# State space layer: last B matrices behind the tokens, tables in one piece on GpSimd, taps ahead of the second values, second turn between two products

## The chip, the cores and the metric

One core of a Trainium2 chip runs the whole program. The time is device microseconds (us) of one execution. The engines are TensorE (PE in the profile; PEld is its weight load), VectorE (DVE), ScalarE (ACT), GpSimd (POOL) and SyncE (SP). SP computes nothing here; it issues most of the DMAs, ACT and POOL issue some of their own. Each engine runs its instructions in the order in which they stand, so an instruction that waits holds up all behind it.

## The reference

Four residual layers over 256 tokens of width 1024, float32. Each layer has a token mixer, a cross-attention to 256 memory tokens and a gated MLP. Layer 2 (of 0 to 3) is the one that the change touches; its mixer is a diagonal complex state space model of 64 groups with 16 channels and 64 states each:

```python
def s5_mixer(h, a_re, a_im, log_dt, b_re, b_im, c_re, c_im, d, w_glu):
    ...
    b_bar = ((a_bar - 1.0) / lam)[..., None] * lax.complex(b_re.astype(f32), b_im.astype(f32))
    ...
    def chunk_step(state, u_blk):
        bu = jnp.einsum('bcgi,gpi->bcgp', u_blk.astype(jnp.complex64), b_bar)
        a_seq = jnp.broadcast_to(a_bar, bu.shape)
        _, xs = lax.associative_scan(_lin_rec_combine, (a_seq, bu), axis=1)
        xs = xs + a_pow[None] * state[:, None]
        y = jnp.real(jnp.einsum('bcgp,gip->bcgi', xs, c_mat))
        return xs[:, -1], y
    ...
    y = jax.nn.gelu(y).astype(h.dtype)
    val, gate = jnp.split(y @ w_glu, 2, axis=-1)
    return val * jax.nn.sigmoid(gate)
```

The memory's keys and values of the same layer (`mem_n @ wkv`) don't depend on the tokens.

## The kernel before, in words

**Products.** A float32 product is made of three matmuls on a high and a low part of both operands (`mm3`, L65 to L67). A weight therefore comes as `raw` (a tile of 1 MB in a ring of three buffers, DMA issued by SP at L88), is rounded by ACT into `whi` (L70) and the rest taken by DVE, or where the plan says `g` by POOL, into `wlo` (L71). The same two lines split every activation: `kh`/`kl`, `vh`/`vl`, `ah`/`al`.

**The state space layer.** Its matrices depend on no token and are built during the layers before, and kept in DRAM: `blD` (B, in four parts), `caD` (C times powers of A, four parts) and `tD` (taps of the convolution inside a block of eight tokens, four parts; `s5_spread`, L916, is the last copy that makes a part of it, two DMAs on POOL's queue for each part). With the tokens in hand `s5_mixer` (L933) does, in this order: the normalized tokens `u` go through eight DMAs of 128 KB into another layout, `uc` (four issued by SP, four by ACT, L962); they are reordered (`ur`, L986), transposed on PE and copied to `v` (L991, ACT and DVE in turn); PE multiplies them with B (`bl`, L1004) into the states' inputs `S` (L1008), transposes these into `SX` (L1030), and DVE scans over them: eight steps inside blocks (L1050 to L1061), then the carry over the blocks with the tables `tab8` (L1069, L1071), which POOL makes (`s5_eighths`, six L680 to L685 a round, L930). PE adds the taps (`taps_u`, L1080) and the carried states (`carry`, L1106) in four PSUM banks; the skip term (`uc` times `db`, L993 on POOL) is added on DVE (L1115), then Gelu (L1117, ACT), the turn back by PE (`turn`, L1123) with its split (L1126 ACT, L1127 DVE), and the GLU product (L1151) with eight weights of 1 MB. There are two halves of channels: `gelu(0)`, `turn(0)` give every second chunk of 128 channels, `gelu(1)`, `turn(1)` the others.

**What fills the waits.** The cross-attention's K (`k0` to `k3`) and V (`v0`, `v1`) products of the same layer are placed into the mixer by a table of names (`self.plan`, L1318 to L1325) and the calls of `self.fill`. `v0` stands at `scan0` and `v1` at `scan1`; a `+` only loads. v0's two PSUM banks are freed when DVE has taken `vl`.

**What sets the order.** A scheduler places each engine's instructions; `with self.behind(x)` keeps the instructions in the block behind `x` on the engine of `x`, and on no other engine. SP's DMAs use eight semaphores in turn, so that a DMA is issued only when the one that had its semaphore before has landed.

Of the kernel before, what the change touches and what calls it, by code (L numbers as in the profile page):

```python
# [36 lines left out]
class Trunk:  # L37
# [871 lines left out]
    def s5_spread(self, mm):  # L909

        if mm == 0:
            self.tD = self.dram.tile([4, P, 2, 8, P], F32, name="tD")
        kd = self.kD[:]
        for par in range(2):
            src = bass.AP(tensor=kd.tensor, offset=kd.offset + (2 * mm + par) * 256 * 240, ap=[[16, 8], [240 * 8, 16], [240, 8], [1, P]])
            self.nc.gpsimd.dma_start(self.tD[mm, :, par].rearrange("(s j) a k -> s j a k", s=8), src)  # L916

    def s5_eighths(self, sp):

        g = self.nc.gpsimd  # L920
        t = sp.tile([P, 3, GP, 8], F32, name="tab8")
        tmp = sp.tile([P, GP, 4], F32, name="tmp8")
        re, im = t[:, 0], t[:, 2]
        g.tensor_copy(re[:, :, 0], self.a8[:, 0, :])
        g.tensor_copy(im[:, :, 0], self.a8[:, 2, :])
        for by in (1, 2, 4):
            b = lambda y: y[:, :, by - 1 : by].to_broadcast([P, GP, by])
            new, old = slice(by, 2 * by), slice(0, by)
            self.cmul(g, re[:, :, new], im[:, :, new], re[:, :, old], im[:, :, old], b(re), b(im), tmp[:, :, 0:by])
        g.tensor_scalar_mul(t[:, 1], im, -1.0)  # L930
        return t

    def s5_mixer(self, l, sp):  # L933
        nc, a = self.nc, self.a
# [17 lines left out]
        for tt in range(TT):  # L952
            r = rs[tt]
            firsts = []
            for nh, f in enumerate((nc.vector.tensor_scalar_mul, nc.scalar.mul)):
                s = slice(512 * nh, 512 * (nh + 1))
# [11 lines left out]
        db = sp.tile([P, 2, 256], F32, name="db")  # L968
        with self.behind(last.ins):
            for i, row in enumerate((a["s5_d"][0], a["mix_norm_g"][l])):  # L970
                nc.sync.dma_start(db[:, i, :], bass.AP(tensor=row.tensor, offset=row.offset, ap=[[256, 4], [0, 32], [1, 256]]))
        with self.behind(self.powed):
            land(2, nc.gpsimd)
            land(3, nc.gpsimd)
            tab8 = self.s5_eighths(sp)
            nc.gpsimd.tensor_mul(db[:, 0, :], db[:, 0, :], db[:, 1, :])
        self.late = firsts
        self.fill("u")
        self.after = [chain, chain + [last.ins]]
        self.fill("u1")  # L980
        self.late = ()
# [103 lines left out]
        self.late = steps[-1:]  # L1085
        taps_u(0)
        taps_u(1)
        self.fill("scan1")
        self.late = ()
        for mm in (2, 3):  # L1090
            landed = taps_land(mm)
            taps_u(mm)

        def carry(mm):
            pool, tag = ((self.big, "xs"), (self.raw, "raw"), (self.raw, "raw"), (self.acts, "ah"))[mm]
            ou = pool.tile([P, 2, 4, 2, P], F32, tag=tag, name="ou")
            with self.behind(landed):
                nc.sync.dma_start(ou[:].rearrange("p m q x k -> p m (q x) k"), self.caD[:, 2 * mm : 2 * mm + 2])
            for m2 in range(2):
                m = 2 * mm + m2  # L1100
# [18 lines left out]
        def turn(h, yh):  # L1119
# [8 lines left out]
            return last  # L1128

        carry(0)  # L1130
        carry(1)
        y0, g0 = gelu(0)
        yT = self.act_pair()
        carry(2)
        done = carry(3)
        with self.behind(done):
            t0 = turn(0, y0)
        y1, _ = gelu(1)
        src = a["s5_w_glu"][0].rearrange("(q h p) n -> p h q n", p=P, h=2)
        for nh in range(2):  # L1140
            acc = self.accs() if nh else [self.bank() for _ in range(4)]
            for kh in range(2):
                for gate in (1, 0):
# [3 lines left out]
                    for tt in range(TT):  # L1147
                        for k in range(4):
                            c = 2 * k + kh
                            s = slice(tt * P, (tt + 1) * P)  # L1150
                            self.mm3(acc[2 * gate + tt][:], (yT[0][:, c, s], yT[1][:, c, s]), w(k, slice(0, 512)), c == 0, c == DC - 1)  # L1151
                if nh == 0 and kh == 0:
                    turn(1, y1)
            sgs = sp.tile([P, TT, 512], F32, tag="g", name="sg")
# [134 lines left out]
    def run(self, layers=range(DEPTH), parts="mcf"):  # L1289
# [14 lines left out]
        for l in layers:  # L1304
# [13 lines left out]
            elif l % 3 == 2:  # L1318
# [3 lines left out]
                self.plan((l, "u"), l, "k1 k2 k3")  # L1322
                self.plan((l, "u1"), l, "+v0dg")
                self.plan((l, "scan0"), l, "v0")
# [97 lines left out]
```

## Time and profile before

| | before |
|---|---|
| median of 3 runs | 1481.85 us (1478.66 to 1484.84) |
| the profiled execution | 1482.43 us, span 1480.7 us |
| mean granted TensorE clock | 0.982 |
| PE, DVE, ACT, POOL busy | 1426.4, 1096.5, 839.3, 124.3 us |
| the chain that ended last | PE 79%, DVE 9%, DMA 6%, ACT 3% |
| DMA | 279.74 MB, mean 189 GB/s |

All times below are microseconds from the start of the span. The mixer of layer 2 begins near 776 and its GLU product ends near 911. Between 700 and 800 PE is busy for 93.6 of 100 us, from 800 to 900 for 83.2 of 100 at a mean granted clock of 0.88; from 900 to 1400 for 97.3 to 100 of each 100.

### The profile page before, as it was taken

What the parts mean: (1) busy time and instruction counts of PE and PEld (TensorE: products, weight loads), DVE (VectorE), ACT (ScalarE), POOL (GpSimd) and SP (SyncE); (2) the same over time, 40 slices, a digit from 0 to 9 for tenths busy, and PEclk for the clock granted to TensorE, in tenths of its full rate; (3) what the DMA queues carried; (4) which work ended last, traced back from release to release, by engine and by line L of the source; (5) the groups of instructions that cost most, each with busy time, mean ns of one, the idle gap of its engine ahead of it and who ended that gap; (6) DMA issues with size and microseconds to landing.
All of it is one profiled execution on the core that took longest, in us unless ns stands there. A gap on an engine that the chain in (4) does not pass through costs nothing.

```text
span 1480.7 us, 25386 instructions
## 1 busy us (share of the span) xinstructions
PE 1426.4 (96%) x10354; PEld 1316.4 (89%) x10354; DVE 1096.5 (74%) x1722; ACT 839.3 (57%) x1351; POOL 124.3 (8%) x128
## 2 busy tenths in 40 slices
PE   7999999998999999999997789999999999999997
PEld 7897999998998989999987668999999999899996
DVE  6969888767886577978783857678677776677675
ACT  7654655547895455645453256565555565565553
POOL 3401000000000000111103500000000030000000
PEclk9999999999999999999998989999999999999999
DMA  7667656645444545776758675455555563465551
GB/s 261 229 164 220 222 199 206 219 135 166 151 149 161 187 148 191 250 225 221 235 192 234 238 233 170 158 171 199 183 187 182 178 210 136 143 220 171 189 181 43
DMA packets 205681, 279.74 MB, mean 189 GB/s; under 512 B 23740, under 2 KB 163132, under 8 KB 203644
## 3 DMA queue, kind: packets, MB, share of 16 engines
q1 hardware_dynamic: 198556, 260.46, 53.0%
q0 software_dynamic: 6432, 17.13, 3.5%
q8 instruction: 81, 1.33, 0.4%
q10 hardware_dynamic: 576, 0.52, 0.1%
q14 instruction: 36, 0.29, 0.1%
HBM read 264.24 MB, written 16.94 MB: 190 GB/s over the span
## 4 chain that ended last, share of the span: by engine, by line
PE 79%; DVE 9%; DMA 6%; ACT 3%; issue 1%; POOL 0%; SPq 0%; DVEq 0%; POOLq 0%; ACTq 0%
PE u L66 10%; PE u L67 10%; PE u L65 10%; PE mm L66 7%; PE mm L65 7%; PE mm L67 7%; PE acc L65 7%; PE acc L66 7%; PE acc L67 7%; DMA raw<-in_ffn_w_up_dram 3%; DVE wlo L71 2%; DMA raw<-in_xa_wkv_dram 2%; ACT whi L70 1%; DVE ug L1261 1%; DMA raw<-in_s_w_glu_dram 1%
## 5 line engine op out<-in xcount | busy, mean ns | idle before, releaser
L71 DVE TENSOR_TENSOR wlo<-raw,whi 128x1024 fp32r<-128x1024 f32 x430 | 519.3, 1220 | 157.0 <-ACT whi L70 148.4
L70 ACT CAST whi<-raw 128x1024 fp32r<-128x1024 f32 (+1 forms) x450 | 460.1, 1045 | 198.8 <-DMA raw<-in_ffn_w_up_dram 55.3
L65 PE MATMUL u<-ah,whi 128*128 128x256 f32 x1408 | 400.6, 285 | 1.7 <-DVE ug L1261 1.3
L66 PE MATMUL u<-al,whi 128*128 128x256 f32 x1408 | 399.8, 284 | 0.4 <-DVE al L71 0.4
L67 PE MATMUL u<-ah,wlo 128*128 128x256 f32 x1408 | 399.5, 284 | 0.0
L65 PEld LDWEIGHTS u<-ah,whi 128*128 128x128 f32 x1408 | 271.2, 193 | 6.3 <-issue 2.5
L66 PEld LDWEIGHTS u<-al,whi 128*128 128x128 f32 x1408 | 271.2, 193 | 3.4 <-DVE al L71 0.9
L67 PEld LDWEIGHTS u<-ah,wlo 128*128 128x128 f32 x1408 | 271.2, 193 | 0.0
L1261 DVE SCALAR_TENSOR_TENSOR ug<-u,cwT,ug 128x255 f32<-128x255 f32 x352 | 168.5, 480 | 101.3 <-ACT ug L1259 96.2
L1259 ACT ACTIVATE ug<-u,cwT 128x256 f32<-128x256 f32 x176 | 99.0, 563 | 185.6 <-PE u L67 125.0
L65 PE MATMUL acc<-whi,gg 128*128 128x512 f32 x352 | 138.0, 392 | 0.0
L66 PE MATMUL acc<-wlo,gg 128*128 128x512 f32 x352 | 137.9, 392 | 0.0
L67 PE MATMUL acc<-whi,gg 128*128 128x512 f32 x352 | 136.9, 389 | 0.0
L66 PE MATMUL mm<-al,whi 128*128 128x256 f32 x384 | 109.9, 286 | 0.1
L65 PE MATMUL mm<-ah,whi 128*128 128x256 f32 x384 | 109.8, 286 | 0.0
L67 PE MATMUL mm<-ah,wlo 128*128 128x256 f32 x384 | 109.4, 285 | 0.0
L176 POOL TENSOR_TENSOR r<-v,mhalf 128x1 f32<-128x1 f32 x28 | 22.7, 813 | 810.5 <-DVE v L172 678.7
L67 PEld LDWEIGHTS acc<-whi,gg 128*128 128x128 f32 x352 | 66.1, 188 | 14.4
L65 PEld LDWEIGHTS acc<-whi,gg 128*128 128x128 f32 x352 | 66.4, 189 | 11.7
L66 PEld LDWEIGHTS acc<-wlo,gg 128*128 128x128 f32 x352 | 66.4, 189 | 10.7
L66 PEld LDWEIGHTS mm<-al,whi 128*128 128x128 f32 x384 | 74.6, 194 | 0.8 <-DVE al L71 0.6
L65 PEld LDWEIGHTS mm<-ah,whi 128*128 128x128 f32 x384 | 74.6, 194 | 0.3 <-ACT ah L70 0.2
(355 smaller groups left out, 2564.9 us busy)
## 6 DMA issues: line engine op xcount, KB each, us to landing
raw<-in_ffn_w_up_dram SPq DMA_DIRECT2D x88, 1024.0 KB
raw<-in_ffn_w_down_dram SPq DMA_DIRECT2D x44, 1024.0 KB
raw<-in_xa_wkv_dram SPq DMA_DIRECT2D x30, 1024.0 KB
raw<-in_xa_wq_dram SPq DMA_DIRECT2D x16, 1024.0 KB
raw<-in_xa_wo_dram SPq DMA_DIRECT2D x16, 1024.0 KB
raw<-in_sb_w_qkv_dram SPq DMA_DIRECT2D x12, 1024.0 KB
raw<-in_s_w_glu_dram SPq DMA_DIRECT2D x8, 1024.0 KB
raw<-in_sb_w_o_dram SPq DMA_DIRECT2D x4, 1024.0 KB
```

The source lines that it names most:

```text
L65: mm(out, lh, rh, start=start, stop=False)
L66: mm(out, lh, rl, start=False, stop=False)
L67: self.multiplied = mm(out, ll, rh, start=False, stop=stop).ins
L70: x = self.nc.scalar.copy(hi, src)
L71: y = (eng or self.nc.vector).tensor_sub(lo, src, hi.bitcast(F32))
L176: self.powed = nc.gpsimd.tensor_tensor(r[:], v[:], self.mhalf[:], ALU.pow).ins
L1259: nc.scalar.activation(u[:, s, :], out, AF.Identity, bias=cw[3], scale=cw[2])
L1261: nc.vector.scalar_tensor_tensor(u[:, s, sh:], out[:, : T - sh], cw[2 - sh], u[:, s, sh:], ALU.mult, ALU.add)
```

## The change

Six edits, all in the mixer of layer 2:

- The last two parts of B (`land(2)`, `land(3)`) are issued by SP behind the token DMAs, ahead of `db`; before, POOL issued them.
- POOL makes the tables without a break, then the product of `db`, then issues both DMAs of the last `s5_spread`; the halves of a `+v0dg` load that POOL splits come behind these (`u2` in place of `u1`).
- The loads of taps 2 and 3 are issued ahead of v1's weights, and all four `taps_u` stand ahead of the v1 product; before, two of them stood behind it.
- The four loads of `caD` (`ou`) are issued together ahead of the first carry, the second of them into a tile of `acts` in place of `raw`.
- `turn(0)` stands behind `carry(2)`; before, behind `carry(3)`.
- `turn(1)` stands behind the first of the two products of the first GLU half (`gate` 1); before, behind both.

```diff
@@ s5_spread, s5_eighths
-            self.nc.gpsimd.dma_start(self.tD[mm, :, par].rearrange("(s j) a k -> s j a k", s=8), src)
+            self.spread = self.nc.gpsimd.dma_start(self.tD[mm, :, par].rearrange("(s j) a k -> s j a k", s=8), src).ins
...
-        g.tensor_scalar_mul(t[:, 1], im, -1.0)
+        self.eighths = g.tensor_scalar_mul(t[:, 1], im, -1.0).ins
@@ s5_mixer
         with self.behind(last.ins):
+            land(2)
+            land(3)
             for i, row in enumerate((a["s5_d"][0], a["mix_norm_g"][l])):
                 nc.sync.dma_start(db[:, i, :], ...
         with self.behind(self.powed):
-            land(2, nc.gpsimd)
-            land(3, nc.gpsimd)
             tab8 = self.s5_eighths(sp)
-            nc.gpsimd.tensor_mul(db[:, 0, :], db[:, 0, :], db[:, 1, :])
+        with self.behind(self.eighths):
+            spread_after = nc.gpsimd.tensor_mul(db[:, 0, :], db[:, 0, :], db[:, 1, :]).ins
         self.late = firsts
         self.fill("u")
         self.after = [chain, chain + [last.ins]]
-        self.fill("u1")
+        with self.behind(spread_after):
+            self.fill("u1")
+        with self.behind(self.spread):
+            self.fill("u2")
...
         self.late = steps[-1:]
-        taps_u(0)
-        taps_u(1)
+        for mm in (2, 3):
+            landed = taps_land(mm)
+        for mm in range(4):
+            taps_u(mm)
         self.fill("scan1")
         self.late = ()
-        for mm in (2, 3):
-            landed = taps_land(mm)
-            taps_u(mm)
-
-        def carry(mm):
-            pool, tag = ((self.big, "xs"), (self.raw, "raw"), (self.raw, "raw"), (self.acts, "ah"))[mm]
+
+        ous = []
+
+        def carried_land(mm):
+            pool, tag = ((self.big, "xs"), (self.acts, "al"), (self.raw, "raw"), (self.acts, "ah"))[mm]
             ou = pool.tile([P, 2, 4, 2, P], F32, tag=tag, name="ou")
             with self.behind(landed):
                 nc.sync.dma_start(ou[:].rearrange("p m q x k -> p m (q x) k"), self.caD[:, 2 * mm : 2 * mm + 2])
+            ous.append(ou)
+
+        def carry(mm):
+            ou = ous[mm]
...
+        for mm in range(4):
+            carried_land(mm)
         carry(0)
         carry(1)
         y0, g0 = gelu(0)
         yT = self.act_pair()
-        carry(2)
-        done = carry(3)
+        done = carry(2)
         with self.behind(done):
             t0 = turn(0, y0)
+        carry(3)
         y1, _ = gelu(1)
...
-                if nh == 0 and kh == 0:
-                    turn(1, y1)
+                    if (nh, kh, gate) == (0, 0, 1):
+                        turn(1, y1)
@@ run
-                self.plan((l, "u1"), l, "+v0dg")
+                self.plan((l, "u2"), l, "+v0dg")
```

The order that the scheduler makes of it differs only in this mixer; ahead of it and from the end of its GLU on, the same instructions stand in the same order on every engine. Line numbers of the changed program are 2 to 11 higher here (L986 is L990, L991 L995, L1008 L1012, L1016 L1020, L1030 L1034, L1098 L1103).

SP, from the token DMAs to the GLU's weights (`bl`: B, `tu`: taps, `ou`: the carry's matrices, `raw<-in_xa_wkv_dram`: weights of v0 and v1). Before:

```order
L962 DMA uc<-u 16x8x256 x4
L971 DMA db<-in_s_d_dram 128x1x256
L971 DMA db<-in_mix_norm_g_dram 128x1x256
L88 DMA raw<-in_xa_wkv_dram 128x4x512 x2
L1016 DMA tu<-tD 128x2048
L88 DMA raw<-in_xa_wkv_dram 128x4x512
L1016 DMA tu<-tD 128x2048
L88 DMA raw<-in_xa_wkv_dram 128x4x512
L1016 DMA tu<-tD 128x2048 x2
L1098 DMA ou<-caD 128x2048 x4
L88 DMA raw<-in_s_w_glu_dram 128x4x512 x3
```

And with the change:

```order
L962 DMA uc<-u 16x8x256 x4
L940 DMA bl<-blD 128x2048 x2
L973 DMA db<-in_s_d_dram 128x1x256
L973 DMA db<-in_mix_norm_g_dram 128x1x256
L88 DMA raw<-in_xa_wkv_dram 128x4x512 x2
L1020 DMA tu<-tD 128x2048 x4
L88 DMA raw<-in_xa_wkv_dram 128x4x512
L1103 DMA ou<-caD 128x2048
L88 DMA raw<-in_xa_wkv_dram 128x4x512
L1103 DMA ou<-caD 128x2048 x3
L88 DMA raw<-in_s_w_glu_dram 128x4x512 x4
```

Two B parts stand between the tokens and `db`; all four tap loads stand ahead of both weights of v1, which stood among them; the `ou` loads stand between and behind these weights.

POOL, behind the norm's last root (`tab`, `tmp`: the tables; the rounds of L680 to L685 go on below the piece). Before:

```order
L940 DMA bl<-blD 128x2048 x2
L924 COPY tab_8533<-a_1589 128x32
L925 COPY tab_8533<-a_1589 128x32
L916 DMA tD<-kD 128x8x128
L680 TENSOR_TENSOR tab_8533<-tab_8533 128x32
L681 TENSOR_TENSOR tmp_8534<-tab_8533 128x32
L683 TENSOR_TENSOR tab_8533<-tab_8533 128x32
L976 TENSOR_TENSOR db<-db 128x256
L682 TENSOR_TENSOR tab_8533<-tab_8533,tmp_8534 128x32
L71 TENSOR_TENSOR wlo<-raw,whi 128x1024
L684 TENSOR_TENSOR tmp_8534<-tab_8533 128x32
```

With the change, the end of the tables and what follows:

```order
L685 TENSOR_TENSOR tab_8533<-tab_8533,tmp_8534 128x32x4
L930 TENSOR_SCALAR tab_8533<-tab_8533 128x256
L977 TENSOR_TENSOR db<-db 128x256
L916 DMA tD<-kD 128x8x128 x2
L71 TENSOR_TENSOR wlo<-raw,whi 128x1024 x2
L997 TENSOR_TENSOR uc<-uc,db 128x2048
L1039 MEMSET X 128x64
L71 TENSOR_TENSOR wlo<-raw,whi 128x1024 x4
```

The tables moved ahead of the product of `db` and of every `wlo`; the first spread DMA moved from the third place behind the table's start to behind that product, the second now follows it at once.

ACT, from the token's reordering to the scan. Before:

```order
L986 COPY ur<-uc 128x512 x2
L991 COPY v<-mm 128x512
L70 CAST whi<-raw 128x1024 x2
L991 COPY v<-mm 128x512
L1008 COPY S<-mm 128x512
L70 CAST whi<-raw 128x1024 x2
L1008 COPY S<-mm 128x512
L1030 COPY SX<-mm 128x8x32
```

And with the change:

```order
L990 COPY ur<-uc 128x512 x2
L995 COPY v<-mm 128x512 x2
L1012 COPY S<-mm 128x512 x2
L70 CAST whi<-raw 128x1024 x2
L1034 COPY SX<-mm 128x8x32 x4
```

The `whi` of v0's weights moved behind ACT's copies of `v` and `S`. On DVE the two `wlo` of the same weight moved from ahead of its `S` copies to between its `SX` copies and the scan's first step.

## The prediction

> **What bounds it now.** The page's busy shares (PE 96%) say nothing about one stage, so I read the stretches first, cut where the waits fall: the state space mixer from its last K product (792) to the end of its GLU (911). Columns are busy time (and count) of PE, PEld, DVE, ACT and POOL, then granted clock, DMA share and GB/s.
>
> ```profile
> 792.00:813.00 21.00, 12.27 (x166) 10.61 (x165) 8.36 (x13) 9.62 (x16) 6.41 (x8) 0.76 0.84 244
> 813.00:847.00 34.00, 29.57 (x267) 23.77 (x273) 29.45 (x48) 7.84 (x10) 20.18 (x20) 0.90 0.64 233
> 847.00:876.00 29.00, 20.15 (x299) 15.79 (x284) 16.70 (x17) 15.53 (x16) 0.00 (x0) 0.91 0.87 295
> 876.00:911.00 35.00, 35.00 (x147) 28.68 (x147) 17.82 (x22) 14.07 (x20) 0.23 (x1) 0.93 0.50 159
> ```
>
> PE idles 8.7, 4.4 and 8.9 us there, and its clock is below full beside each hole: that is all the change can win. PE's waits between 785 and 900, longest first, name the holes (total, times, longest); the row at 806 below adds 2.2 us behind ACT's v copy:
>
> ```profile
> PE mm L990 <- ACT ur L986: 5.2, 1, 5.2
> PE mm L65 <- DVE vl L71: 4.4, 2, 2.4
> PE acc L1106 <- DMA ou<-caD: 3.5, 1, 3.5
> ```
>
> **Tokens and S.** The timelines of ACT and PE (start, duration, what; in brackets the idle time before it and what ended it), then the DMA queues from 780 to 798 (packets, MB, share of 16 engines):
>
> ```profile
> 792.63 0.58 ACT L70 CAST kh<-mm 128x512 fp32r<-128x512 f32 x1 [5.17 <-PE mm L67]
> 797.10 1.14 ACT L986 COPY ur<-uc 128x512 f32<-128x512 f32 x2 [3.89 <-DMA uc<-u]
> 803.60 1.99 ACT L70 CAST whi<-raw 128x1024 fp32r<-128x1024 f32 x2 [4.08 <-DMA raw<-in_xa_wkv_dram]
> 805.50 0.58 ACT L991 COPY v<-mm 128x512 f32<-128x512 f32 x1
> ...
> 797.78 3.68 PE L990 MATMUL mm<-ident,ur 128*128 128x128 f32 x16 [5.18 <-ACT ur L986]
> 806.13 3.55 PE L1004 MATMUL mm<-bl,v 128*32 128x128 f32 x64 [2.21 <-ACT v L991]
> 809.61 1.97 PE L1028 MATMUL mm<-ident,S 128*128 128x128 f32 x16
> ...
> q0 software_dynamic: 560, 2.63, 47.8%
> q10 hardware_dynamic: 576, 0.52, 12.3%
> ```
>
> The eight token transfers (uc, 1 MB) land at 797.1. Half of them went by q10 and took 12.3% of 18 us, 2.2 us of all engines, so all take 4.4. The bl transfers on GpSimd's queue (q0) took 8.6 us of the same time. With bl behind the tokens, uc lands between 785 and, if nothing changes, 797.1. I take any time before 792.6: then the third kh copy (792.63 + 0.58) is the next gate and ur starts at 793.2, 3.9 us earlier; the bounds are 3.9 and 0.
>
> In the Trainium skill, DMA: Bandwidth & Descriptors says that every DMA engine takes its queue rows in turn, packet by packet (Queues, rings and completion order), which agrees with q0 and q10 sharing the 18 us above. [...]
>
> The second v copy stood behind whi, which waited 4.08 us for a weight. ACT now runs v, v, S, S ahead of whi. Transposes at 793.8, 2.0 us at full clock (L1028's 1.97; the 3.68 is at half), the copies, and the second half of the S product starts near 797.2 instead of 806.13. It needs bl 2 and 3; these issue as tokens land, from about 786. The first row below is how long the two took today (the summary of tile bl); the others are DVE's timeline:
>
> ```profile
> DMA to landing us min/median/max: 6.7/9.0/11.3
> ...
> 804.68 2.36 DVE L71 TENSOR_TENSOR wlo<-raw,whi 128x1024 fp32r<-128x1024 f32 x2 [2.50 <-ACT whi L70]
> 813.35 1.22 DVE L1050 COPY X<-SX 128x256 f32<-128x256 f32 x1 [1.02 <-ACT SX L1030]
> 827.23 0.67 DVE L71 TENSOR_TENSOR vl<-mm,vh 128x512 fp32r<-128x512 f32 x1
> 831.40 0.51 DVE L1058 TENSOR_TENSOR two<-X,sc 128x192 f32<-128x192 f32 x1
> 842.43 0.62 DVE L1071 TENSOR_TENSOR X<-X,two 128x448 f32<-128x448 f32 x1
> ```
>
> So bl lands at 793 to 798: just in time. On SP it stands ahead of db and of v0's weights, 2 MB or 7.1 us at the 295 GB/s of the third stretch; but the same 2 MB shared the engines with them today, so I have v0's first weight land between 796 and today's 803.6. From 806.13 to the scan (813.35) is 7.2 us with two whi in it; DVE's two wlo (2.36), now ahead of the scan, run beside ACT's SX copies. Scan start: 797.2 + 7.2, 804.5 (8.8 earlier). If the weight lands no sooner than 803.6, whi and wlo push it to 808.0 (5.3 earlier).
>
> **Second values.** The v1 product needs v0's banks, freed by vl, and is now also behind all taps. POOL's timeline with the summary of tile tD (how long the spread took to land), then PE's and SP's:
>
> ```profile
> 800.89 0.72 POOL L976 TENSOR_TENSOR db<-db 128x256 f32<-128x256 f32 x1 [17.17 <-DMA db<-in_mix_norm_g_dram]
> 812.98 1.37 POOL L916 DMA_DIRECT2D tD<-kD  x1
> 829.56 2.36 POOL L71 TENSOR_TENSOR wlo<-raw,whi 128x1024 fp32r<-128x1024 f32 x1
> 832.42 0.87 POOL L930 TENSOR_SCALAR tab<-tab 128x256 f32<-128x256 f32 x1
> DMA to landing us min/median/max: 11.3/12.8/14.3
> ...
> 812.91 0.50 PE L65 MATMUL mm<-whi,mgh 128*128 128x512 f32 x1 [1.34 <-ACT SX L1030]
> 824.01 1.95 PE L1080 MATMUL acc<-tu,v 128*32 128x128 f32 x64
> 830.90 0.80 PE L65 MATMUL mm<-whi,mgh 128*128 128x512 f32 x1 [2.44 <-DVE vl L71]
> 844.53 1.95 PE L1080 MATMUL acc<-tu,v 128*32 128x128 f32 x64
> 825.71 0.34 SPq L1016 DMA_DIRECT2D tu<-tD  x1
> ```
>
> In the scan, vl comes 18.05 us (813.35 to 831.40) less two vl, 17 us, after its start: 821.5, first bank 822.2. The chain that I think ends later is on POOL and SP. The tables, whose last piece ends at 833.3 today, just ahead of their first use, run in one piece and cost nothing: they fit in the 17.17 us that POOL stood idle waiting for db. Behind them comes the db product, whose db now stands behind bl on SP: it lands between 794 and today's 800.9; then 0.72 and two spreads of 1.37 (today the second goes out at 812.98), 797.9 to 804.3; landing 11.3 to 14.3 later, 809 to 818.6. SP holds the last taps' load until then, and everything behind it: v1's weights, ou, GLU. Middle: tu(3) issues at 810.7 (825.71 today) and lands 6.7 us later (bl's least, the same 1 MB), 817.4. The v0 product starts near 803.6 with its first wlo, takes 11.1 us (812.91 to 824.01), and three taps 2.9: PE is there at 817.6, so the taps' move costs nothing; without that cover it costs what tu(3) is late. v1's first weight is 1 MB more, 3.6 us at 295 GB/s, then whi 1.0 and POOL's wlo 2.36: v1 starts at 824.4, 6.5 earlier, and no earlier than 822.2; with the late ends, 818.6 + 9.0 + 7.0 = 834.6, 3.7 later than now.
>
> **Carry, first turn.** v1 takes (830.90 to 844.53) 13.6 us as now (its half clock spell included): carry at 838.0; the scan ends at 804.5 + 29.7 = 834.2, and the four ou, now issued ahead, lie under v1, so the 3.5 us wait goes. The timelines from there on, and two stretches with the granted clock (next to the last two numbers):
>
> ```profile
> 846.41 2.03 PE L1106 MATMUL acc<-ou,X 64*32 64x128 f32 x128
> 849.86 1.06 ACT L1117 ACTIVATE uc<-uc 128x1024 f32<-128x1024 f32 x1 [4.64 <-DVE uc L1115]
> 855.42 1.96 PE L1123 MATMUL yt<-ident,uc 128*128 128x128 f32 x8
> 859.06 0.50 PE L65 MATMUL mm<-whi,ah 128*128 128x512 f32 x1 [1.68 <-ACT ah L1126]
> 870.62 1.04 PE L1123 MATMUL yt<-ident,uc 128*128 128x128 f32 x8
> 875.20 0.79 PE L65 MATMUL mm<-whi,ah 128*128 128x512 f32 x1 [1.43 <-ACT ah L1126]
> 875.00:881.00 6.00, 5.80 (x14) 4.54 (x15) 2.62 (x3) 2.28 (x3) 0.00 (x0) 0.50 0.66 183
> 806.00:808.00 2.00, 1.87 (x36) 1.74 (x40) 1.64 (x2) 2.00 (x4) 0.42 (x1) 0.51 0.22 90
> ```
>
> From carry to the end of gelu is 4.5 us (846.41 to 850.92), from the turn to the GLU 3.6: GLU at 838.0 + 8.1 = 846.1, 12.9 earlier.
>
> **Second turn.** It ended at 871.7, the product went on at 875.20 (3.5), and six microseconds at clock 0.50 cost 2.9 more. Between two products, its copies lie under 24 matmuls, 5.8 us (half of 859.06 to 870.62). Gelu 2 stands on ACT behind a GLU weight whose load waits for carry 2 (841 + 6.7 to 9.0, whi, gelu: 850 to 852); the first product ends at 851.9, so the cover barely holds. Without it, up to 3.5 us comes back. I take 6.4.
>
> **Sum.** 12.9 + 6.4 = 19.3 us. Against it one half clock spell, 2.9 us: in the row at 806 a wait of 2.21 us was enough for clock 0.51, and the carry, gelu and first turn still leave gaps of 1 to 2 us. That gives 16.4 off the execution's own 1482.43 (span 1480.7, 1.7 around it), so 1466.0; the execution lay 0.6 over the median of the runs, so against the median 1465 us. From 911 on no engine's order changes, and PE is full there, so what is won stays won.
>
> In the Trainium skill, TensorE: Matmul & The Clock Gate (Part 1) lets the clock fall after an idle window of about 3.4 us. By that the gaps stay at full clock and the sum is 19.3, 1462.5; the trace's 2.21 us speaks against it.
>
> **Rivals.** Data no earlier: the same 16 engines move the same bytes, tokens at 797.1, scan at 808.0. vl frees v1 at 825.7, 5.2 earlier; GLU 11.6 earlier, and with 6.4 - 2.9 the time is 1467. For it: DMA share 0.84 in the first stretch; against: half the bytes were q0's. Late spread: the late ends above, v1 at 834.6, the GLU at 856.3, 2.8 earlier, and with 6.4 - 2.9: 1475.5. For it: db waited 17 us; against: both spreads go out before today's second. Slower: the same chain, longer. GLU comes 13.7 + 13.6 + 8.1 = 35.4 us after tu(3) issues; with 6.4 - 2.9 won later, the two kernels are level when tu(3) issues at 827.3; at 837 the time is 1491. db would have to land after 809; nothing shows that. No effect: some wait that I don't see (a GLU weight, a bank) refills the holes, 1480.
>
> **Chances.** Forecast 0.50, data no earlier 0.15, late spread 0.17, slower 0.08, no effect 0.10. About 0.5% (7.4 us) is what a measurement tells from no change: faster 0.75 (with 0.10 of late spread), same 0.17, slower 0.08. The range goes from 1457 (v1 at 822.2, no half clock at all) to 1478 (late spread, second turn uncovered).
>
> **What would show it.** ur at 793, scan by 805, tu(3) issued before 812, v1 by 825, carry without a wait for ou, GLU near 846, no PE wait at the second turn. I am wrong if SP still waits for tD past 820 or ACT's whi holds the SX copies.

## The result, and the profile after

| | before | changed |
|---|---|---|
| median (range), first comparison, 5 runs each | 1479.22 us (1475.88 to 1484.84) | 1467.85 us (1466.19 to 1470.14) |
| ratio, 95% interval | | 0.9921 (0.9902 to 0.9941) |
| median (range), second comparison, 11 and 6 runs | 1479.15 us (1474.74 to 1485.54) | 1465.39 us (1463.80 to 1469.24) |
| ratio, 95% interval | | 0.9905 (0.9884 to 0.9927) |
| profiled execution: span, mean granted clock | 1480.7 us, 0.982 | 1465.8 us, 0.988 |

The change is 11 to 14 us faster; the forecast was 1465 us. Whether it was right for its reasons is another question, and for that the whole-program times are too coarse. I therefore look at one stage alone: from the start of the last `kh` copy on ACT (792.63 in the first profile of before) to the end of the last addition to `h` of this mixer. Both kernels were profiled twice. The stretches of the stage, in the order before, before again, changed, changed again (columns: start:end, length, busy us and count of PE, PEld, DVE, ACT, POOL, then granted clock, DMA share, GB/s):

```profile
792.63:912.15 119.52, 96.97 (x856) 78.80 (x856) 73.44 (x100) 48.04 (x62) 27.16 (x27) 0.89 0.68 226
```
```profile
791.65:908.27 116.62, 94.74 (x856) 77.45 (x856) 73.62 (x100) 48.14 (x62) 27.21 (x27) 0.88 0.69 232
```
```profile
793.93:897.34 103.41, 89.44 (x856) 73.50 (x856) 73.14 (x100) 48.10 (x62) 22.86 (x12) 0.93 0.78 273
```
```profile
796.83:899.33 102.50, 89.10 (x856) 72.80 (x856) 73.25 (x100) 48.24 (x62) 22.93 (x12) 0.95 0.78 276
```

The stage is 16.1 us shorter in the first pair and 14.1 in the second. What to see here: length less PE busy is PE's idle time, 22.6 and 21.9 us before, 14.0 and 13.4 after, so 8.5 us of waits are gone. The other 5.6 to 7.5 us are PE *busy* time, with the same 856 records on both sides: the same products ran at a higher granted clock (0.88 to 0.89 before, 0.93 to 0.95 after). So 40 to 47% of what the stage won is clock. The clock records of the four traces bear this out: half of the time that PE was busy at clock 0.50 is 11.7, 10.0, 4.7 and 4.1 us, and PE's busy time less that is 85.3, 84.8, 84.7 and 85.0 us, the same on both sides.

The same moments in all four profiles, in us after the last `kh` copy, beside the forecast (its times less 792.63):

| | before | before again | forecast | changed | changed again |
|---|---|---|---|---|---|
| `ur` starts | 4.5 | 5.2 | 0.6 | 0.5 | 0.5 |
| v0 product starts | 20.3 | 19.2 | 11.0 | 14.5 | 14.5 |
| scan starts | 20.7 | 19.6 | 11.9 (at worst 15.4) | 14.9 | 15.0 |
| tu(3) issued | 33.1 | 33.7 | 18.1 (at worst 26.0) | 24.6 | 24.6 |
| v1 runs, its waits behind it | 38.3 | 37.3 | 31.8 | 35.7 | 35.8 |
| carry | 53.8 | 53.0 | 45.4 | 49.4 | 48.5 |
| GLU | 66.4 | 66.8 | 53.5 | 57.0 | 56.1 |
| end of the stage | 119.5 | 116.6 | 103.1 | 103.4 | 102.5 |

The end is where it was forecast, what lies between is not. PE's waits of the changed kernel between 785 and 900, as for before:

```profile
PE mm L65 <- ACT SX L1034: 5.7, 1, 5.7
PE mm L65 <- ACT whi L70: 2.4, 1, 2.4
PE mm L66 <- POOL wlo L71: 1.9, 1, 1.9
...
PE mm L994 <- ACT ur L990: 1.2, 1, 1.2
```

Gone are `ur` (5.2, now 1.2), `vl` (4.4) and `ou` (3.5). New are 5.7 us ahead of the v0 product and 2.4 and 1.9 inside v1. ACT's timeline, with DVE's scan start, names the first:

```profile
793.93 0.58 ACT L70 CAST kh<-mm 128x512 fp32r<-128x512 f32 x1 [5.17 <-PE mm L67]
794.41 1.14 ACT L990 COPY ur<-uc 128x512 f32<-128x512 f32 x2
800.04 0.58 ACT L1012 COPY S<-mm 128x512 f32<-128x512 f32 x1 [1.16 <-PE mm L1008]
804.99 1.99 ACT L70 CAST whi<-raw 128x1024 fp32r<-128x1024 f32 x2 [4.36 <-DMA raw<-in_xa_wkv_dram]
806.89 1.96 ACT L1034 COPY SX<-mm 128x256 f32<-128x256 f32 x4
...
808.87 0.42 DVE L1054 COPY X<-SX 128x256 f32<-128x256 f32 x1 [0.45 <-ACT SX L1034]
```

`ur` no longer waits for the tokens, and ACT has done its copies of `v` and `S` by 800.6 (DVE its own by 801.6). Then ACT stands 4.36 us in `whi` for v0's first weight, with the SX copies behind it in order. POOL and SP, then SP's longest waits for the tap loads and weights:

```profile
802.52 0.72 POOL L977 TENSOR_TENSOR db<-db 128x256 f32<-128x256 f32 x1 [13.30 <-DMA db<-in_mix_norm_g_dram]
803.18 2.68 POOL L916 DMA_DIRECT2D tD<-kD  x2
...
818.49 0.32 SPq L1020 DMA_DIRECT2D tu<-tD  x1
818.92 0.38 SPq L88 DMA_DIRECT2D raw<-in_xa_wkv_dram  x1
823.98 0.38 SPq L88 DMA_DIRECT2D raw<-in_xa_wkv_dram  x1
...
SPq L1020 <- DMA tD<-kD: 14.3, 1, 14.3
SPq L88 <- PE acc L1084: 4.0, 1, 4.0
```

POOL waits for `db` until 802.5, the spreads go out behind it, SP stands 14.3 us for `tD`, and v1's first weight goes out only then; the second waits 4.0 more, until the tap product has freed its ring buffer. PE from there on:

```profile
827.15 0.49 PE L65 MATMUL mm<-whi,mgh 128*128 128x512 f32 x1 [2.35 <-ACT whi L70]
829.59 0.79 PE L66 MATMUL mm<-wlo,mgh 128*128 128x512 f32 x1 [1.94 <-POOL wlo L71]
843.33 2.85 PE L1115 MATMUL acc<-ou,X 64*32 64x128 f32 x186
847.56 0.65 PE L1115 MATMUL acc<-ou,X 64*32 64x128 f32 x26 [1.38 <-issue]
848.14 1.09 PE L1132 MATMUL yt<-ident,uc 128*128 128x128 f32 x8
850.93 0.50 PE L65 MATMUL mm<-whi,ah 128*128 128x512 f32 x1 [0.86 <-ACT ah L1135]
856.98 1.03 PE L1132 MATMUL yt<-ident,uc 128*128 128x128 f32 x8
```

Carry to GLU is 7.6 us (12.7 and 13.9 before), the turns run at full clock (1.09 and 1.03 for eight transposes, 1.96 for the first before), and no wait follows the second turn.

### The profile page after: what moved, and what is told of

Read it like the earlier page. It is cut to its first block, busy times and chain, and to the rows that moved or that the text cites. A ratio compares the mean times of both kernels' runs of the same rounds, so it can differ in the third digit from the quotient of the medians.

```text
span 1465.8 us, 25388 instructions
## 1 busy us (share of the span) xinstructions
PE 1418.3 (97%) x10354; PEld 1311.3 (89%) x10354; DVE 1096.4 (75%) x1722; ACT 839.3 (57%) x1351; POOL 123.3 (8%) x126
## 3 DMA queue, kind: packets, MB, share of 16 engines
q1 hardware_dynamic: 198844, 262.56, 53.8%
## 4 chain that ended last, share of the span: by engine, by line
PE 78%; DVE 10%; DMA 6%; ACT 3%; issue 2%; POOL 0%; SPq 0%; DVEq 0%; POOLq 0%; ACTq 0%
PE u L66 9%; PE u L67 9%; PE u L65 9%; PE mm L66 8%; PE mm L67 8%; PE mm L65 8%; PE acc L65 7%; PE acc L66 7%; PE acc L67 7%; DMA raw<-in_ffn_w_up_dram 3%; DVE wlo L71 3%; DMA raw<-in_xa_wkv_dram 2%; ACT whi L70 2%; DVE ug L1272 2%; DVE h L435 1%
## 5 line engine op out<-in xcount | busy, mean ns | idle before, releaser
L176 POOL TENSOR_TENSOR r<-v,mhalf 128x1 f32<-128x1 f32 x28 | 22.6, 808 | 790.9 <-DVE v L172 678.9
L67 PEld LDWEIGHTS acc<-whi,gg 128*128 128x128 f32 x352 | 66.1, 188 | 14.3
L65 PEld LDWEIGHTS acc<-whi,gg 128*128 128x128 f32 x352 | 66.4, 189 | 11.7
L66 PEld LDWEIGHTS acc<-wlo,gg 128*128 128x128 f32 x352 | 66.4, 189 | 10.8
L65 PE MATMUL mm<-mgh,whi 128*128 128x256 f32 x256 | 73.5, 287 | 1.0 <-ACT whi L70 1.0
```

Source lines behind the costliest of these rows:

```text
L65: mm(out, lh, rh, start=start, stop=False)
L66: mm(out, lh, rl, start=False, stop=False)
L67: self.multiplied = mm(out, ll, rh, start=False, stop=stop).ins
L176: self.powed = nc.gpsimd.tensor_tensor(r[:], v[:], self.mhalf[:], ALU.pow).ins
```

## The experiments

In each the stage was read from one profile and the time from several runs. Ratios are to the kernel before; the stage and its moments are in us after the last `kh` copy.

| kernel | v0 | scan | v1, first | carry | GLU | stage | PE idle | ratio (95%) |
|---|---|---|---|---|---|---|---|---|
| before, again | 19.2 | 19.6 | 34.4 | 53.0 | 66.8 | 116.6 | 21.9 | (one run) |
| changed, again | 14.5 | 15.0 | 33.3 | 48.5 | 56.1 | 102.5 | 13.4 | 0.9905 (0.9884 to 0.9927) |
| second turn only | 18.9 | 19.4 | 34.1 | 52.3 | 64.2 | 113.0 | 21.3 | 0.9968 (0.9955 to 0.9982) |
| copies before weight | 12.1 | 10.5 | 33.2 | 48.4 | 55.9 | 102.4 | 13.1 | 0.9908 (0.9892 to 0.9924) |
| `db` first | 16.3 | 16.7 | 33.9 | 48.8 | 57.4 | 103.8 | 15.0 | 0.9915 (0.9898 to 0.9931) |
| B parts on POOL | 17.5 | 18.0 | 35.3 | 48.0 | 55.9 | 102.3 | 13.8 | 0.9916 (0.9901 to 0.9931) |
| tap in u's buffer | 14.4 | 14.9 | 33.2 | 48.0 | 55.7 | 101.9 | 13.7 | 0.9919 (0.9894 to 0.9944) |
| all four | 12.8 | 11.9 | 31.3 | 43.4 | 54.6 | 101.2 | 12.5 | 0.9901 (0.9881 to 0.9921) |
| taps behind v1 | 14.5 | 15.0 | 32.1 | 46.7 | 58.6 | 105.6 | 14.4 | 0.9932 (0.9919 to 0.9946) |
| first turn behind carry | 14.5 | 14.9 | 33.2 | 48.4 | 56.7 | 106.1 | 15.8 | 0.9929 (0.9912 to 0.9946) |
| B on POOL, order free | 18.2 | 18.6 | 39.1 | 51.7 | 59.2 | 105.7 | 16.0 | 0.9907 (0.9892 to 0.9923) |
| half the bytes | 16.0 | 15.1 | 34.5 | 46.9 | 55.4 | 102.3 | 10.1 | 0.9894 (0.9877 to 0.9910) |

### Both kernels once more

> The kernel before, once more, for a second profile. From the start of the last kh copy (792.63 in the first profile) to the end of the last addition to h of this mixer (912.15) lie 119.5 us before and 103.4 us after the change: 16.1 us, against 11.4 us between the medians. Theory: the stage is stable within 1 us and the rest lies ahead of it, in code that no edit touches (the stage starts at 793 to 797 in the other profiles): 118.5 to 120.5 us here. Rival: the first profile fell on a long stage, and the stage is 3 to 5 us shorter here.

> The changed kernel, once more, for a second profile and more times on one chip. Theory: the same stage 102.5 to 104.5 us long; ratio to the kernel before 0.990 to 0.994. Rival, as above: a stage 2 us or more off, which would make differences of 1 to 2 us between single profiles worth nothing.

Measured: 116.6 and 102.5. The changed kernel's stage repeats within 1 us, that of before does not: 2.9 us, of which 2.2 are PE busy time. So differences of 1 to 2 us between single profiles carry nothing, and part of before's cost is clock that comes and goes. The stage itself starts anywhere between 791.7 and 796.8 in the fourteen profiles; behind it, 567 to 569 us follow in all of them. From the first token DMA to the last `kh` copy it is 12.4 to 12.5 us in every profile, so no edit moves the start. The scatter arises ahead of the mixer, in code that is the same in all: one ACT instruction there starts between 729.1 and 731.3, a later one between 766.2 and 771.4. Why it scatters stays open; it is why the medians and the stages of single profiles need not agree to 3 us.

### The second turn alone

```diff
 (kernel before)
-                if nh == 0 and kh == 0:
-                    turn(1, y1)
+                    if (nh, kh, gate) == (0, 0, 1):
+                        turn(1, y1)
```

> The kernel before, with one edit of the six: the second turn stands between the two products of the first GLU half. Theory (the prediction's step): the 3.5 us wait of PE at the second turn and the half-clock spell behind it (2.9 us) both go, 6.4 us less than before, and no PE wait stands behind the second turn's transposes. Rival one, the clock falls anyway: 3.5 us less. Rival two, the turn's copies are not covered by the other product: 0 to 1 us less. If 6.4 comes out, the other five edits together are worth only some 5 of the 11.4 us between the two kernels.

Measured: 4.7 us less in time (2.7 to 6.7), 6.5 and 3.6 in the stage against the two profiles of before. The GLU's first product and the second turn on PE, then two stretches of that product with the clock (next to the last two numbers):

```profile
858.44 0.80 PE L65 MATMUL mm<-whi,ah 128*128 128x512 f32 x1 [3.18 <-ACT ah L1126]
...
867.05 1.03 PE L1123 MATMUL yt<-ident,uc 128*128 128x128 f32 x8
```
```profile
858.00:861.00 3.00, 2.56 (x6) 2.10 (x7) 3.00 (x3) 3.00 (x4) 0.00 (x0) 0.50 0.90 355
864.00:867.00 3.00, 3.00 (x14) 2.45 (x14) 1.70 (x2) 0.00 (x0) 0.00 (x0) 1.00 1.00 341
```

No wait follows 867.05, so the cover holds. Half clock did not leave the GLU, though: it now follows the 3.18 us wait at the *first* turn. The edit takes the wait away for certain and the spell only if nothing else brings one. It is the one edit of the six that was tried alone on the kernel before, and its worth shows in the times.

### The copies ahead of v0's weight

v0's splits are emitted behind the SX copies and held there; the rest of the order stays.

```diff
+        with self.behind(self.spread, *copied[-2:]):   # the last SX copies on ACT and DVE
+            for f in deferred:                         # the splits of v0's two weights
+                f()
```

> The changed kernel, but ACT and DVE split v0's weights (whi, wlo) behind all SX copies, not ahead of them. In the changed kernel ACT stood 4.4 us in whi for v0's first weight with the SX copies behind it. Theory: the scan starts near 804 instead of 808.9 and the v0 product near 806 instead of 808.4, but v1 still starts when its own weight lands (near 827), since SP issues that weight only behind the last taps' load, and this one waits for tD: 0 to 1 us less than the changed kernel. Rival: the start of the scan or of the v0 product sets the end: 2.3 to 4.5 us less.

DVE's scan start and PE's starts of v0 and v1:

```profile
803.97 0.39 DVE L1067 COPY X<-SX 128x256 f32<-128x256 f32 x1 [1.00 <-ACT SX L1042]
...
805.52 1.22 PE L65 MATMUL mm<-whi,mgh 128*128 128x512 f32 x2 [3.27 <-ACT whi L70]
826.61 0.80 PE L65 MATMUL mm<-whi,mgh 128*128 128x512 f32 x1 [2.84 <-ACT whi L70]
```

The scan came 4.4 us earlier and v0 2.4, and v1 started where it does in the changed kernel, 33.2 after the `kh` copy, now with a longer wait for its weight. The time is the changed kernel's within the intervals. The missed scan start of the forecast was thus not what cost the carry.

### `db` before the tokens

```diff
         land(0)        # the two db loads now stand ahead of this
...
         with self.behind(last.ins):
             land(2)
             land(3)
-            for i, row in enumerate((a["s5_d"][0], a["mix_norm_g"][l])):
-                nc.sync.dma_start(db[:, i, :], ...
```

> The changed kernel, but SP issues the two small db loads with the first B parts, before the tokens, not behind them and two B parts. Theory: the db product on POOL follows the tables at 789 instead of 802.5, both spread DMAs go out by 793 and land by 807, SP no longer stands 14.3 us for tD; the next gate for v1's first weight is its buffer, which POOL's wlo of v0 frees at 816, against the 818.9 of the changed kernel: v1 starts 2 to 3 us earlier and the time is 2 to 3 us less than the changed kernel's. Rival: the spread's 1 MB then shares the engines with the tokens and B parts (full there already), what comes earlier on one side is late on the other: 0 to 2 us more.

SP's issue of v1's first weight and PE's start of v0:

```profile
819.00 0.38 SPq L88 DMA_DIRECT2D raw<-in_xa_wkv_dram  x1
...
812.92 0.80 PE L65 MATMUL mm<-whi,mgh 128*128 128x512 f32 x1 [6.57 <-ACT SX L1044]
```

The last `kh` copy starts at 796.67 here, so v1's weight went out at 22.3 instead of 25.0, as reckoned, and PE no longer waited for it. But v0 started 1.7 us later (its weight came at 11.6 instead of 11.1, and two of DVE's SX copies stand behind `wlo` in this kernel), and v1 not before 33.9: the rival. Two gates, each about as late as the other, hide each other's removal.

### B's last parts on POOL's queue

```diff
         with self.behind(last.ins):
-            land(2)
-            land(3)
...
         with self.behind(self.powed):
+            land(2, nc.gpsimd)
+            land(3, nc.gpsimd)
```

> The changed kernel, but POOL issues the last two B parts on its own queue beside the tokens, as before the change; ACT's and DVE's order is held to that of the changed kernel. The prediction priced the tokens' earlier landing at 3.9 us. Theory now: the tokens land 3 to 4 us later (ur near 797 to 798), but v0's first weight, which the same engines bring, lands no later than now (805), and the v0 product and v1 start where they do now: 0 to 1 us more than the changed kernel. Rival (the prediction's step): all that follows the tokens is 3.9 us later, and the time 3 to 4 us more.

> The changed kernel with the last two B parts on POOL's queue again, as in the run with B on POOL, but ACT's and DVE's order is no longer held: the splits of v0's weights go back ahead of the second v copy and between the S copies, as in the kernel before. Theory: the order on ACT, not the queue of B, is what brought the v0 product forward (14.5 after the last kh copy; 17.5 with B on POOL and the order held; 19.2 and 20.3 before): v0 comes at 19 to 20, the scan at 19.5 to 20.5, the carry at 50.5 to 52, and the time is 2 to 4 us more than the changed kernel's. Rival: the order is worth as little as the queue: within 1 us of the changed kernel.

With the order held: ACT's `ur`, then the end of the scan on DVE:

```profile
796.56 1.14 ACT L998 COPY ur<-uc 128x512 f32<-128x512 f32 x2 [2.83 <-DMA uc<-u]
...
839.86 0.62 DVE L1090 TENSOR_TENSOR X<-X,two 128x448 f32<-128x448 f32 x1
```

The tokens are 2.9 us later than in the changed kernel, v0 and scan 3.0 (the order is not quite the same: DVE's `wlo` stands ahead of its SX copies here, behind them in the changed kernel). Yet the carry stands at 48.0, no later than in the changed kernel: here the scan ends just ahead of it (840.5 and 841.1), there v1's weights set it. B's place behind the tokens, the edit that the title names first, earned nothing at the end of the stage.

With the order free, v0 came only 0.7 us later still (18.2, below the expected 19), the carry at 51.7 as expected, but for another reason. DVE's first scan step and what POOL did then:

```profile
812.89 3.91 DVE L1054 COPY X<-SX 128x256 f32<-128x256 f32 x1 [1.03 <-ACT SX L1034]
...
811.78 4.60 POOL L997 TENSOR_TENSOR uc<-uc,db 128x2048 f32<-128x2048 f32 x1
```

A copy of 0.42 us took 3.91 and ended 0.4 us behind POOL's product. The time shows no loss (1466.14 us, 0.9907), and the profiled execution lay at the upper end of its runs: what ACT's order alone is worth stays open between 0 and 3.4 us.

### The third taps in u's buffer

```diff
-... = ((self.acts, "ah"), (self.acts, "al"), (self.raw, "raw"), (self.raw, "raw"))[mm]
+... = ((self.acts, "ah"), (self.acts, "al"), (self.big, "xs"), (self.raw, "raw"))[mm]
             tu = ...
...
-            with self.behind(landed):
+            with self.behind(self.sent):          # v1's second weight
                 nc.sync.dma_start(ou[:] ...
```

> The changed kernel, but the third part of the taps lands in the buffer of u, no longer in the ring of three buffers of the weights, and both v1 weights are issued ahead of the first ou. In the changed kernel SP held v1's second weight 4.0 us until the tap product had freed that ring buffer; PE then waited 1.9 us for this weight's wlo inside v1 at half clock. Theory: the second weight is issued right behind the first, the inner wait and its half clock go, and the carry starts 3 to 4 us earlier: 3 to 4 us less than the changed kernel. Rival: v1's second half is bound by POOL's wlo (4.7 us for a pair) or by the DMA rate, 0 to 1 us less.

SP's issue of v1's two weights and PE inside v1:

```profile
816.99 0.93 SPq L88 DMA_DIRECT2D raw<-in_xa_wkv_dram  x2
...
827.73 0.80 PE L66 MATMUL mm<-wlo,mgh 128*128 128x512 f32 x1 [1.94 <-POOL wlo L71]
```

The second weight went out with the first, yet the 1.94 us wait is the *first* weight's `wlo`, and it stayed: the carry came 0.5 to 1.4 us earlier, the rival's number.

### All four together, and with half the bytes

> The changed kernel with four edits together: db loaded before the tokens; the third B part loaded before the tokens too (into the buffer that later holds the states); SX copies ahead of the splits of v0's weights; the third taps in u's buffer with both v1 weights ahead of ou. Theory, in times after the last kh copy: v0's first weight at 9 to 10 (11.1 now), v0 product at 11 (14.5), scan at 10.5 (14.9), tu(3) issued by 15 (24.6), v1 at 28, where vl frees its banks (33.2), carry at 41.5 (49.4), GLU at 49 (57.0): 7 to 8 us less than the changed kernel. Rival: the 16 DMA engines are full from 784 on whatever the order, the weights land no sooner: 2 to 3 us less, as with the single edits.

> The kernel with the four edits together, but the taps and ou are loaded by half (the even one of each pair of matrices, used twice, so the skip of four MB changes what is computed; the number and shape of PE's products stay). Theory: what is left of the stage is bound by the 16 DMA engines, full from 784 to 820 and from 830 to 840, and not by the order: 4 MB less at 390 to 404 GB/s are up to 10 us of their time; v0's first weight, tu and ou land earlier, the 4.0 us wait inside the carry goes, and the stage from the last kh copy to the last addition to h (101.9 with the four edits) is 4 to 7 us shorter. Rival: it is bound by the chain of scan, vl and PE's own work: 0 to 1.5 us shorter.

With the four edits (`db`, third B part early, copies first, taps in u's buffer) PE's timeline reads, with two rows of the DMA view, the instruction queue's between 841 and 842 and the sum between 843 and 844:

```profile
825.28 0.47 PE L65 MATMUL mm<-whi,mgh 128*128 128x512 f32 x1 [0.66 <-DVE vl L71]
837.40 2.84 PE L1128 MATMUL acc<-ou,X 64*32 64x128 f32 x185 [0.37 <-DVE X L1088]
844.21 1.09 PE L1128 MATMUL acc<-ou,X 64*32 64x128 f32 x27 [3.97 <-issue]
...
q8 instruction: 1, 0.02, 6.2%
...
DMA packets 0, 0.00 MB, mean 0 GB/s; under 512 B 0, under 2 KB 0, under 8 KB 0
```

v1 waits only 0.33 us for a weight's `wlo`, and the carry begins the moment the scan ends: 43.4, 5 to 6 us earlier than in the changed kernel. The edits also have a price that I had not seen: with `db` and a third B part issued ahead, ACT issues its last token DMA only at 789.97, 8 us behind its first one, and `ur` starts at 2.0 instead of 0.5. In the middle of the carry PE stands 3.97 us for nothing that the profile shows, a half-clock spell follows, and the GLU comes 1.5 to 2.4 us earlier; 0.9901 is not distinguishable from 0.9905. The expectation for the half bytes took this wait for one on `ou`. It was not: between 843 and 844 the DMA view has no packet at all, so `ou` had landed by then. With 4 MB less the wait was 1.6 us and PE's idle time 2.4 us less, but PE's busy time 92.11 us instead of 88.70:

```profile
794.97:897.22 102.25, 92.11 (x856) 75.15 (x856) 72.64 (x100) 48.40 (x62) 20.59 (x9) 0.92 0.70 230
```

The stage was no shorter. But a half-clock spell lay over the transposes and the S product in this profile (2.0 to 8.8 us after the `kh` copy; `v0` and scan came 3.2 us later than with all bytes), and half clock cost 3.2 us more of PE's busy time than with all bytes. Without that the stage would be some 2 us shorter, an estimate: less than the 4 to 7 expected, more than the 0 to 1.5 of the rival. That the DMA rate binds what is left is thereby not borne out, nor ruled out for 2 us; carry stands 31.5 to 31.8 us behind the scan's start in both, which speaks for the scan.

### Taps, and the first turn, put back

```diff
 (taps behind v1)
-        for mm in (2, 3):
-            landed = taps_land(mm)
-        for mm in range(4):
-            taps_u(mm)
+        taps_u(0)
+        taps_u(1)
         self.fill("scan1")
         self.late = ()
+        for mm in (2, 3):
+            landed = taps_land(mm)
+            taps_u(mm)
```

> The changed kernel with one of its edits undone: the loads and products of taps 2 and 3 stand behind v1's weights and product again. Times after the last kh copy. Theory: the edit earned nothing, since it put tu(3), which waits for tD, and the ring buffer of tu(2) ahead of v1's weights; without it v1's weights come early, v1 starts near 33 as now, when vl has freed the banks, and runs without an inner wait; two tap products (2 us) then stand ahead of the carry, which comes at 47.5 to 49 (48.5 and 49.4 in the two profiles of the changed kernel): the time stays within 1.5 us of the changed kernel's. Rival (the prediction's step): v1 comes back by the 3 to 6 us that the step was priced at, and the time is 3 to 6 us more.

```profile
841.73 2.85 PE L1116 MATMUL acc<-ou,X 64*32 64x128 f32 x186
848.71 0.66 PE L1116 MATMUL acc<-ou,X 64*32 64x128 f32 x10 [4.13 <-issue]
```

The last `kh` copy starts at 795.00, so the carry comes at 46.7: with taps 2 and 3 *behind* v1 it is 1.7 to 2.7 us earlier than in the changed kernel. All is lost again in the carry (4.13 us, at the same place as above) and in a half-clock spell behind it (53.2 to 60.0), and the stage ends 2.2 to 3.1 us later; the ratio is 0.9932. Theory for v1, neither theory for the end.

```diff
 (first turn behind the fourth carry)
-            pool, tag = ((self.big, "xs"), (self.acts, "al"), (self.raw, "raw"), (self.acts, "ah"))[mm]
+            pool, tag = ((self.big, "xs"), (self.raw, "raw"), (self.raw, "raw"), (self.acts, "ah"))[mm]
...
-        done = carry(2)
+        carry(2)
+        done = carry(3)
         with self.behind(done):
             t0 = turn(0, y0)
-        carry(3)
```

> The changed kernel, but the first turn stands behind the fourth carry again and the second ou lands in the weights' ring again; the ou loads keep their place on SP. From carry to GLU the two profiles of the changed kernel have 7.6 us, those before 12.7 and 13.9. Theory: the 5 to 6 us came from the ou loads being issued ahead (PE waited 3.5 us for one); PE waits for gelu at the first turn anyway and the fourth carry fills part of that: carry to GLU 8 to 9 us, the time 0 to 1.5 us more. Rival: the order of turn and carry earned it: carry to GLU 11 us or more, 3 us more.

Carry to GLU 8.4 us: 0.8 more, so the order of turn and carry is worth little here. Of the 5.1 to 6.2 us between the two kernels, 4.3 to 5.5 remain, of which PE's wait for `ou` before the change was 3.5 and 2.7. But the stage is 2.7 to 3.6 us longer, most of it in the GLU. SP's issue of the first GLU weight, PE's waits at the GLU's start and the clock behind them:

```profile
836.49 0.38 SPq L88 DMA_DIRECT2D raw<-in_s_w_glu_dram  x1
```

```profile
848.73 0.50 PE L65 MATMUL mm<-whi,ah 128*128 128x512 f32 x1 [1.65 <-ACT ah L1136]
851.23 0.50 PE L65 MATMUL mm<-whi,ah 128*128 128x512 f32 x1 [1.30 <-ACT whi L70]
```
```profile
852.00:855.00 3.00, 3.00 (x9) 2.32 (x8) 2.52 (x3) 2.96 (x4) 0.00 (x0) 0.50 0.81 268
```

1.65 and 1.30 us of waiting in place of one of 0.86 were followed by half clock in the product. The run undoes two things at once. The wait of 1.30 us is one for a GLU weight: with the second `ou` in the weights' ring again SP waits 5.8 us for POOL to free its buffer, and the first two GLU weights go out 44.5 and 50.4 us after the `kh` copy instead of 38.0 and 44.4. So the tile is its likelier cause, not the order; no run separates them.

Two of the six edits were not undone alone: the tables in one piece on POOL with both spreads behind them, and the four `ou` loads issued together. What each of them is worth by itself stays open.

## Why the prediction came out

**Tokens: mechanism right, size wrong, worth nothing.** `ur` started where forecast. But a queue's share was no price: the tokens' ACT half, which had 2.2 us of all engines beside B, had 4.7 when nearly alone (last section). And the run with B on POOL shows that the 3 us they came earlier were worth nothing at the carry.

**S and scan: the stated bound came true.** v0's first weight was put between 796 and 803.6; it came at 11.1 after the `kh` copy, 803.7 on the scale of before. The scan then had to start at 15.4, and did at 14.9. One of the two signs that I had named for being wrong, `whi` holding the SX copies, came true. v0 came 3.5 us later than forecast; putting the copies ahead of the weight brought 2.4 of that back and, by itself, nothing at the carry.

**Second values: the step that failed.** I let `db` land from 794 to 800.9 and took tu(3)'s issue in the middle, 810.7. `db` landed no earlier than in before: SP issued its second row 5.7 and 4.6 us ahead of the `kh` copy instead of 0.8 and 0.3, but behind 2 MB of B, and POOL's product started at 8.6 in both profiles against 8.3 and 8.5. So tu(3) was issued at 24.6 instead of 18.1, near the late end of the range. v1's first weight then came faster than priced, so v1 ran 3.9 us later than forecast and not 6.5. I had not seen that the taps' new place makes v1's second weight wait 4.0 us for a ring buffer; without that wait the carry was 0.5 to 1.4 us earlier, no more than single profiles differ by. And "the taps' move costs nothing" does not hold at the carry, which is 1.7 to 2.7 us earlier with the taps back behind v1, though the stage then ends later.

**Carry, first turn: right.** 8.1 us forecast from carry to GLU, 7.6 measured, without a wait for `ou`. GLU came 9.4 and 10.7 us earlier in the two pairs, 12.9 forecast.

**Second turn: right as a wait, half right as a clock.** The wait went. The spell behind it, 2.9 us, stood in only one of the two profiles of before; by time the edit alone gives 4.7, forecast 6.4.

**The sum: near, by errors that offset each other.** For the stage 16.4 us were forecast, 16.1 and 14.1 measured; between the medians it is 11.4 and 13.8. That the time itself, 1465, comes nearer than the win is luck: the three runs of before from which I took it off have a median 2.6 us above that of all five. Within the stage the GLU term was 2.2 to 3.5 us too large. On the other side I had charged one new half-clock spell of 2.9 us, so that the clock would give about nothing; in fact PE's busy time fell by 5.6 to 7.5 us. The times do not tell the forecast from "data no earlier" (1467): the medians are 1467.85 and 1465.39. The moments do: the tokens did come earlier, but the scan's start is that rival's, and tu(3)'s issue is nearly that of "late spread", whose 1475.5 and whose v1 at 42.0 after the `kh` copy (35.7 measured) are ruled out.

**The signs.** `ur`, the carry without a wait for `ou` and the second turn without a wait came as named. The scan by 805, tu(3) before 812, v1 by 825 and the GLU near 846 did not: they came at 808.9, 818.5, 829.6 (behind its waits) and 850.9. SP's wait for `tD` ended just short of the 820 that I had named for being wrong.

## What to carry to other kernels

When several gates end within 2 us of each other, a single edit shows nothing: ask for each moved start what else ends just behind it, and price the edit by the second latest. A wait on the matmul engine costs its length and, where a half-clock spell follows, 1.6 to 3.1 us more in the kernel before (once 5.1), so the gaps that went were worth more here than their own length. Compare a stage from one anchor to another in two profiles of each kernel before reading 2 us out of it.

## What the runs showed of the hardware

**Half-clock spells come and go.** In the first profile of before the second turn left a wait of 3.5 us and 6 us at clock 0.50 behind it. In the second profile of the same kernel, the wait there and two stretches, over the first turn and behind the second:

```profile
874.09 0.50 PE L65 MATMUL mm<-whi,ah 128*128 128x512 f32 x1 [1.45 <-ACT ah L1126]
...
855.00:858.00 3.00, 2.22 (x13) 1.57 (x8) 2.52 (x4) 2.14 (x3) 0.00 (x0) 0.50 0.96 274
878.00:881.00 3.00, 3.00 (x15) 2.49 (x14) 0.48 (x1) 1.86 (x3) 0.00 (x0) 1.00 0.92 294
```

Here the spell lies over the first turn and none follows the second. In the clock records of the fourteen traces every spell within the stage lasts 3.41 us or two, three or four times that. Gaps of 2.35 and 1.94 us (v1 of the changed kernel) and of 1.65 and 1.30 us (first turn put back) brought spells, single ones of 0.86 and 1.45 us did not. The Trainium skill, TensorE: Matmul & The Clock Gate (Part 1), calls the window free-running, so that the same kernel can differ from run to run; the two profiles of before agree with that. A single gap as long as its idle window of about 3.4 us was not needed here.

**The token transfers stay slow when they are nearly alone.** The stretch in which the tokens had the engines nearly to themselves (changed kernel), and their ACT half's row in the DMA view, from 782 to 793:

```profile
785.93:788.93 3.00, 3.00 (x27) 3.00 (x26) 0.14 (x1) 0.59 (x1) 2.73 (x6) 1.00 1.17 124
...
q10 hardware_dynamic: 576, 0.52, 42.4%
```

The engines count as full (1.17) at 124 GB/s. The same 576 packets took 42.4% of 11 us, 4.7 us of all engines, against 12.3% of 18 us, 2.2, beside B's transfers before the change, although from the first of these packets to the last it was 8.7 us and 10.8 us: the time in the packets of one queue was no measure here of what a transfer takes. The Trainium skill, DMA: Bandwidth & Descriptors (Why small descriptors are slow), has copies inside SBUF free of the penalty on small descriptors; these 1 KB rows, sixteen partitions wide at the target, are not fast, whatever the cause.

**PE stops at one place in the carry.** In every profile it pauses after the 185th to 187th carry matmul, 0.4 to 4.1 us, put down to "issue". In all fourteen one packet of 16 KB on the instruction queue starts 2.3 to 2.9 us ahead of PE's going on, however long the pause, and in the 2 us ahead of the packets of the two longest pauses the DMA engines moved 320 to 400 GB/s. That PE waits there for its next instructions, and that their transfer comes late behind data, fits this, but no run separated it.

**A DVE copy waited out a POOL product**, 3.91 us for 0.42, in one profile. The Trainium skill, SBUF — State Buffer (Who interferes with whom), describes a port pair that such a copy and GpSimd lock against each other for a whole instruction; the end of the copy 0.4 us behind POOL's agrees.
